# Inverting the diagonal blocks of the delta rule by block doubling instead of rank-one steps

## The chip, the core and the metric

The kernel runs on one core of a Trainium2 chip. The metric is the device time of one execution in microseconds. TensorE (PE) multiplies matrices, with weight loads (PEld) beside it; VectorE (DVE) and ScalarE (ACT) do the elementwise work; GpSimd (POOL) issues some DMAs; SyncE (SP) issues most of them.

## The reference, cut to what matters

Two transformer blocks run one after the other on 512 tokens of width 1024. The first block's mixer has a gated delta rule with four heads; the rest (projections, attention, two MLPs) the change does not touch. For each chunk of a head a unit lower triangular system is solved:

```
k_beta = k * beta
v_beta = v * beta
m = jnp.where(strict, jnp.einsum('bhnid,bhnjd->bhnij', k_beta, k) * lmask, 0.0)
a = m + jnp.eye(c, dtype=f32)
rhs = jnp.concatenate([v_beta, k_beta * jnp.exp(decay)[..., None]], axis=-1)
sol = lax.linalg.triangular_solve(a, rhs, left_side=True, lower=True, unit_diagonal=True)
u_c = sol[..., :dv]
w_c = sol[..., dv:]
...
def step(state, inp):
    qk_i, q_dec_i, k_dec_i, u_i, w_i, cd_i = inp
    v_new = u_i - jnp.einsum('bhck,bhkv->bhcv', w_i, state)
    o = jnp.einsum('bhck,bhkv->bhcv', q_dec_i, state) + jnp.einsum('bhij,bhjv->bhiv', qk_i, v_new)
    state = state * cd_i[..., None, None] + jnp.einsum('bhck,bhcv->bhkv', k_dec_i, v_new)
    return state, o
```

The kernel uses chunks of 128 tokens, so a head has four systems of 128x128, and it forms the inverse of `a` itself.

## The kernel before, in words

Weights come from HBM in tiles of 128x1024, are split into a rounded high part (ACT, L256) and the rest (VectorE, L257), and every projection is made of three matmuls (L275 to L277). Loads are issued on SP (L253); a load waits until the casts of an earlier tile have freed its buffer.

`deltanet` writes the four heads down between the projections that feed them and others that don't depend on them: the output projection of the other branch (`do_wa`) and the key and value projections of the memory attention (`next(mem)`, weights `xa_wk` and `xa_wv`). After head 3, `w_out1` (weights `w_out_b`) needs the output of all four heads; before it, `fins[3]` transposes head 3's output (L743) and splits it (L307, L308).

The order of the instructions on each engine is fixed when the program is built: a planner walks through the program with modelled durations and gives a free engine the earliest-written instruction that it takes to be ready. An engine then runs its list in that order. So instructions of two heads and of projections alternate on VectorE, and a change of one instruction can move others.

In `dn_head` the inverse is built in stages. L635 masks the scaled Gram matrix `M` to its diagonal blocks of 16. A product with an identity (L631) packs them into PSUM, and ACT copies them into `Lp` (L641), 16 columns for each of 128 rows and 4 chunks. Four DMAs on SP (L648), one a chunk, move them so that each of 32 partitions holds one whole block of 16x16 (`Lb`). There the inverse `Tb` starts as the identity (two memsets, L645 and L646), and 15 rank-one steps follow, two VectorE instructions each (L651 multiplies, L653 subtracts), every one dependent on the last. Four DMAs on SP (L655) bring `Tb` back to the rows, and L657 spreads it into `T_`. From there two more levels (16 to 32 and 32 to 64) and a last join to 128 are made with matmuls, VectorE and ACT, then the four chunks are run in sequence (L700 to L738). `Ob`, the scratch of the steps, lies in the tile `Mo`, which L635 fills with another mask when the steps are done.

Besides, from head 3 on, `sum_jobs` has ACT issue copies of 256 KB from HBM to HBM (L218) and GpSimd add to them (L222).

Of the kernel before, what the change touches and what calls it, by code (L numbers as in the profile page):

```python
# [12 lines left out]
AF = mybir.ActivationFunctionType  # L13
ALU = mybir.AluOpType
AX = mybir.AxisListType
# [50 lines left out]
class Kern:  # L66
# [491 lines left out]
    def dn_head(self, h, q, k, v, pr, gate, yb_h, yb_l):  # L558
        nc, mp = self.nc, self.mp
        V, TT = nc.vector, nc.vector.tensor_tensor  # L560
# [29 lines left out]
        r = self.rsqrt(mp, s2, 8, "dr")  # L590
# [34 lines left out]
        flat = lambda ap: ap.rearrange("p b c -> p (b c)")  # L625
        split = lambda ap, c: ap.rearrange("p b (o c) -> p b o c", c=c)

        def mmp(lhs, rhs, n):
            ps = psc()
            for b in range(NB):  # L630
                nc.tensor.matmul(ps[:, b * n:(b + 1) * n], lhs[:, b], rhs(b), start=True, stop=True)  # L631
            return vn_(ps, n)
# [5 lines left out]
        Md = masked(b4("dT"), "bd16")  # L638
        psL = mmp(Md, lambda b: self.bmask("ident16")[:, 0, :16], 16)
        Lp, Rp = b32("dVb")[:, :, :16], b32("dY")[:, :, :16]  # L640
        nc.scalar.copy(Lp, psL)  # L641
        Vt, Mo = b4("dV"), b4("dA" + e, 1)
        bl = lambda t, o: t[0:32].rearrange("p b c -> p (b c)")[:, o:o + 256].rearrange("p (r c) -> p r c", r=16)
        Lb, Tb, Ob = bl(Vt, 0), bl(Vt, 256), bl(Mo, 0)
        V.memset(Tb, 0.0)  # L645
        V.memset(flat(Tb)[:, 0::17], 1.0)  # L646
        for b in range(NB):
            nc.sync.dma_start(Lb[8 * b:8 * b + 8], Lp[:, b])  # L648
        for j in range(15):
            n, m = 15 - j, j + 1  # L650
            nc.vector.tensor_tensor(out=Ob[:, :n, :m], in0=Lb[:, m:, j:m].broadcast_to([32, n, m]),  # L651
               in1=Tb[:, j:m, :m].broadcast_to([32, n, m]), op=ALU.mult)
            nc.vector.tensor_tensor(out=Tb[:, m:, :m], in0=Tb[:, m:, :m], in1=Ob[:, :n, :m], op=ALU.subtract)  # L653
        for b in range(NB):
            nc.sync.dma_start(Rp[:, b], Tb[8 * b:8 * b + 8])  # L655
        T_ = b32("dTb")
# [1 line left out]
           in1=split(self.bmask("half"), 16).broadcast_to([P, NB, 2, 16]), op=ALU.mult)  # L658
        Md = masked(Md, "m16")
        masked(Mo, "m32")  # L660
        for lv, Mx in ((16, Md), (32, Mo)):
# [4 lines left out]
               in1=split(self.maskb("bd32"), 32), op=ALU.mult)  # L666
# [31 lines left out]
        o = b4("do", 1)  # L698
# [855 lines left out]
```

## Time and profile before

| | |
|---|---|
| median of 3 runs | 1709.44 us (1708.92 to 1714.01) |
| profiled execution | 1707.82 us, its span 1706.0 us |
| TensorE busy | 1681.1 us, 99% |
| VectorE, ScalarE, GpSimd busy | 1216.6, 822.0 and 66.3 us |
| mean granted TensorE clock | 0.996 |
| HBM read, written | 201.59 and 35.65 MB |

The span is the time from the first to the last instruction; the execution adds what lies around it. Times on the timelines count from the span's start. The ends of matmuls are modelled, so successive matmuls overlap in the listing; the distance between their starts is the rate.

### The profile page before, as it was taken

How to read it: one execution, taken by the hardware profiler on the slowest of the kernel's cores; microseconds unless marked ns; L12 is line 12 of the kernel's file. 1: busy time of each engine (PE TensorE's matmuls, PEld its weight loads, DVE VectorE, ACT ScalarE, POOL GpSimd, SP SyncE). 2: the span in 40 equal slices, each digit the busy share in tenths (PEclk: the TensorE clock that was granted, in tenths of full speed). 3: DMA queues.
4: the chain of work that ended last, by engine and by line, in shares of the span. 5: the costliest groups of instructions: out<-in, count | busy, mean ns of one | idle time of the engine just before them, and what ended most of it. 6: DMA issues, size and time to landing. Idle time of an engine off the chain costs nothing.

```text
span 1706.0 us, 25979 instructions
## 1 busy us (share of the span) xinstructions
PE 1681.1 (99%) x9924; PEld 1456.4 (85%) x9924; DVE 1216.6 (71%) x2574; ACT 822.0 (48%) x1462; POOL 66.3 (4%) x86
## 2 busy tenths in 40 slices
PE   9999999999999999999999999999999999999998
PEld 8988898877898989888988887788888989898987
DVE  6988885756686868688845569865556767676875
ACT  5355654544444444454444457654244444444553
POOL 0200001000000000000000000000000000000000
PEclk9999999999999999999999999999999999999999
DMA  6321357436546464423333332334464454643331
GB/s 202 100 75 53 104 162 182 112 93 171 122 134 165 131 167 131 130 93 107 100 91 101 99 87 68 93 87 118 116 188 128 132 166 131 166 131 123 100 111 50
DMA packets 81948, 205.64 MB, mean 121 GB/s; under 512 B 13088, under 2 KB 14240, under 8 KB 81824
## 3 DMA queue, kind: packets, MB, share of 16 engines
q1 hardware_dynamic: 62672, 169.29, 31.9%
q0 software_dynamic: 9216, 16.78, 6.9%
q10 hardware_dynamic: 9936, 17.91, 3.8%
q8 instruction: 78, 1.28, 0.3%
q14 instruction: 46, 0.38, 0.1%
HBM read 201.59 MB, written 35.65 MB: 139 GB/s over the span
## 4 chain that ended last, share of the span: by engine, by line
PE 88%; DVE 7%; ACT 2%; issue 1%; DMA 1%; SPq 0%; ACTq 0%; DVEq 0%
PE psd L276 21%; PE psd L275 21%; PE psd L277 21%; PE x L275 5%; PE x L276 5%; PE x L277 5%; DVE wl L257 1%; PE c L578 1%; PE c L631 1%; PE lg L1308 1%; PE po L1335 1%; ACT wh L256 1%; DVE acc L318 1%; DVE S L418 1%; PE m L1229 1%
## 5 line engine op out<-in xcount | busy, mean ns | idle before, releaser
L277 PE MATMUL psd<-S,wl 128*128 128x512 f32 (+1 forms) x1256 | 485.1, 387 | 0.6 <-DVE wl L257 0.5
L275 PE MATMUL psd<-S,wh 128*128 128x512 f32 (+1 forms) x1256 | 484.3, 386 | 0.8 <-ACT S L307 0.8
L276 PE MATMUL psd<-S,wh 128*128 128x512 f32 (+1 forms) x1192 | 459.6, 386 | 0.2
L275 PEld LDWEIGHTS psd<-S,wh 128*128 128x128 f32 x1256 | 237.2, 189 | 46.2 <-ACT S L307 1.0
L277 PEld LDWEIGHTS psd<-S,wl 128*128 128x128 f32 x1256 | 237.2, 189 | 45.8 <-DVE wl L257 1.4
L257 DVE TENSOR_TENSOR wl<-wr,wh 128x1024 fp32r<-128x1024 f32 (+2 forms) x160 | 192.0, 1200 | 107.6 <-ACT wh L256 107.0
L276 PEld LDWEIGHTS psd<-S,wh 128*128 128x128 f32 x1192 | 225.0, 189 | 43.4 <-DVE S L305 1.4
L256 ACT CAST wh<-wr 128x1024 fp32r<-128x1024 f32 (+2 forms) x160 | 164.0, 1026 | 160.3 <-PE psd L276 112.3
L276 PE MATMUL psd<-wl,S 128*128 128x256 f32 (+2 forms) x480 | 135.6, 283 | 0.3 <-DVE wl L257 0.3
L275 PE MATMUL psd<-wh,S 128*128 128x256 f32 (+2 forms) x480 | 135.5, 283 | 0.0
L277 PE MATMUL psd<-wh,S 128*128 128x256 f32 (+2 forms) x480 | 135.2, 282 | 0.0
L275 PE MATMUL x<-S,wh 128*128 128x256 f32 x452 | 128.0, 285 | 3.1 <-DVE x_fm L947 2.9
L276 PE MATMUL x<-S,wh 128*128 128x256 f32 x452 | 126.5, 281 | 0.0
L277 PE MATMUL x<-S,wl 128*128 128x256 f32 x452 | 126.0, 280 | 0.0
L276 PE MATMUL psd<-S,whx 128*128 128x512 f32 (+1 forms) x296 | 108.9, 368 | 0.1
L275 PE MATMUL psd<-S,whx 128*128 128x512 f32 (+1 forms) x296 | 107.9, 366 | 0.0
L277 PE MATMUL psd<-S,wlx 128*128 128x512 f32 (+1 forms) x296 | 107.2, 362 | 0.0
L947 DVE TENSOR_TENSOR x_fm<-x_fm,x 128x256 f32<-128x256 f32 x192 | 78.8, 417 | 27.3 <-PE x L277 27.1
L276 PEld LDWEIGHTS psd<-wl,S 128*128 128x128 f32 x480 | 90.4, 188 | 1.0 <-DVE wl L257 0.5
L275 PEld LDWEIGHTS psd<-wh,S 128*128 128x128 f32 x480 | 90.3, 188 | 0.4
L277 PEld LDWEIGHTS psd<-wh,S 128*128 128x128 f32 x480 | 90.5, 188 | 0.0
L275 PEld LDWEIGHTS x<-S,wh 128*128 128x128 f32 x452 | 84.9, 188 | 6.1 <-DVE x_fm L947 2.9
(465 smaller groups left out, 3180.4 us busy)
## 6 DMA issues: line engine op xcount, KB each, us to landing
wrx<-in_ffn_w_dram SPq DMA_DIRECT2D x32, 512.0 KB
wrx<-in_w_up_dram SPq DMA_DIRECT2D x20, 512.0 KB
wr<-in_w_in_qk_dram SPq DMA_DIRECT2D x16, 512.0 KB
sums_ffn_w<-in_ffn_w_dram ACTq DMA_DIRECT2D x32, 256.0 KB
wr<-in_ffn_w_dram SPq DMA_DIRECT2D x16, 512.0 KB
sums_w_down<-in_w_down_dram ACTq DMA_DIRECT2D x32, 256.0 KB
wr<-in_w_in_v_dram SPq DMA_DIRECT2D x12, 512.0 KB
wr<-in_w_up_dram SPq DMA_DIRECT2D x12, 512.0 KB
```

Source lines behind the costliest of these rows:

```text
L256: self.last_cast = nc.scalar.copy(hi[:, c], raw[:, c])
L257: nc.vector.tensor_tensor(out=lo[:, c], in0=raw[:, c], in1=hi[:, c].bitcast(F32), op=ALU.subtract)
L275: mm(ps, ah, bh, start=first, stop=False, skip_group_check=more)
L276: mm(ps, ah, bl, start=False, stop=False, skip_group_check=more)
L277: self.last_mm = mm(ps, al, bh, start=False, stop=last, skip_group_check=more)
L318: nc.vector.tensor_tensor(out=acc, in0=acc, in1=sq, op=ALU.add)
L418: nc.vector.tensor_scalar(out=d, in0=d, scalar1=ag[:, j, 0:1], scalar2=r[:, j:j + 1], op0=ALU.subtract, op1=ALU.mult)
L578: nc.tensor.matmul(blk(ps, b), lhs(b), rhs(b), start=True, stop=True)
L631: nc.tensor.matmul(ps[:, b * n:(b + 1) * n], lhs[:, b], rhs(b), start=True, stop=True)
L947: TT(out=x[n][t], in0=x[n][t], in1=ps, op=op)
L1229: nc.tensor.matmul(pX[:, :W], PT[:, tt], va[:, tt], start=True, stop=True)
L1308: nc.tensor.matmul(ps[:, i, K0:], qs[:, 2 * e2 + i, cs], kd[:, w, kc], start=(w == 0), stop=(w == 1))
```

## The change

The copy of the packed blocks gets the sign (-1). Of the four DMAs that lay out the blocks, two are now issued on SP and two on ACT. The 15 steps are replaced: blocks of 1 are joined to 2 by a copy of the entries below the diagonal, and then blocks of n = 2, 4 and 8 are joined to 2n, for all pairs of a block at once. For a pair, T21 = T22 (-L21) T11: each of the two products is a multiplication into `w` (n x n x n terms a pair, in n or m instructions, or one for n = 8) and a sum over the last axis. The right-hand factor is read transposed, so from element to element it moves by one row of 16 numbers. The four DMAs back stay on SP.

```
-        nc.scalar.copy(Lp, psL)
+        nc.scalar.activation(Lp, psL, AF.Copy, scale=-1.0)
         Vt, Mo = b4("dV"), b4("dA" + e, 1)
...
         for b in range(NB):
-            nc.sync.dma_start(Lb[8 * b:8 * b + 8], Lp[:, b])
-        for j in range(15):
-            n, m = 15 - j, j + 1
-            nc.vector.tensor_tensor(out=Ob[:, :n, :m], in0=Lb[:, m:, j:m].broadcast_to([32, n, m]),
-               in1=Tb[:, j:m, :m].broadcast_to([32, n, m]), op=ALU.mult)
-            nc.vector.tensor_tensor(out=Tb[:, m:, :m], in0=Tb[:, m:, :m], in1=Ob[:, :n, :m], op=ALU.subtract)
+            (nc.sync, nc.scalar)[b % 2].dma_start(Lb[8 * b:8 * b + 8], Lp[:, b])
+        V.tensor_copy(flat(Tb)[:, 16::34], flat(Lb)[:, 16::34])
+        for n in (2, 4, 8):
+            m = 8 // n
+
+            def part(t, o, i, j):
+
+                c = o + 17 * n * i if i == j else o + 16 * n
+                v = rows(t)[:, c:c + 34 * n * (m - 1) + 17 * n - 16]
+                return bass.AP(v.tensor, v.offset, [list(v.ap[0]), [34 * n, m], [16, n], [1, n]])
+
+            L21, T11, T22, T21 = part(Vt, 0, 1, 0), part(Vt, 256, 0, 0), part(Vt, 256, 1, 1), part(Vt, 256, 1, 0)
+            w = rows(Mo)[:, :m * n ** 3].rearrange("p (q i j k) -> p q i j k", q=m, i=n, j=n)
+            for lhs, rhs, out in ((L21, T11, L21), (T22, L21, T21)):
+                rT = rhs.rearrange("p q k j -> p q j k")
+                if n < m:
+                    for i in range(n):
+                        TT(out=w[:, :, i], in0=lhs[:, :, i:i + 1].broadcast_to([32, m, n, n]), in1=rT, op=ALU.mult)
+                else:
+                    for i in range(m):
+                        TT(out=w[:, i], in0=lhs[:, i].rearrange("p i (o k) -> p i o k", o=1).broadcast_to([32, n, n, n]),
+                           in1=rT[:, i:i + 1].broadcast_to([32, n, n, n]), op=ALU.mult)
+                V.reduce_sum(out=out, in_=w, axis=AX.X)
         for b in range(NB):
             nc.sync.dma_start(Rp[:, b], Tb[8 * b:8 * b + 8])
```

## Rows read from the trace of the kernel before

**Rows 1.** The page, busy time of each engine.
```profile
PE 1681.1 (99%) x9924; PEld 1456.4 (85%) x9924; DVE 1216.6 (71%) x2574; ACT 822.0 (48%) x1462; POOL 66.3 (4%) x86
```

**Rows 2.** Stretches: us, busy us of each engine, granted clock, DMA share, GB/s.
```profile
252.00:256.00 4.00, 4.00 (x37) 4.00 (x36) 4.00 (x21) 2.06 (x6) 0.81 (x1) 1.00 0.81 261
...
264.00:268.00 4.00, 2.72 (x22) 2.32 (x20) 3.24 (x6) 1.63 (x3) 0.47 (x1) 1.00 0.87 211
...
292.00:296.00 4.00, 2.24 (x9) 1.12 (x8) 1.97 (x12) 1.28 (x4) 0.45 (x1) 1.00 0.48 67
296.00:300.00 4.00, 3.22 (x8) 2.48 (x8) 1.34 (x2) 0.84 (x2) 0.00 (x0) 0.51 0.00 0
300.00:304.00 4.00, 4.00 (x13) 3.15 (x12) 3.68 (x6) 4.00 (x7) 0.00 (x0) 0.63 0.15 42
```

**Rows 3.** Timeline of PE: start, us, line, operation, count, idle before and its releaser.
```profile
224.32 1.16 PE L578 MATMUL c<-masks,slg 128*128 128x128 f32 x8 [1.46 <-ACT c L587]
...
267.82 1.08 PE L631 MATMUL c<-dTb,dT 128*128 128x32 f32 x8 [0.96 <-DVE dTb L657]
...
292.74 0.40 PE L277 MATMUL psd<-S,wl 128*128 128x512 f32 x1
294.90 1.20 PE L743 MATMUL c<-masks,do 128*128 128x128 f32 x4 [1.76 <-ACT do L738]
296.88 1.65 PE L275 MATMUL psd<-S,wh 128*128 128x512 f32 x3 [0.78 <-ACT S L307]
298.32 0.63 PE L276 MATMUL psd<-S,wh 128*128 128x512 f32 x1
...
302.99 0.40 PE L277 MATMUL psd<-S,wl 128*128 128x512 f32 x1
```

**Rows 4.** Timeline of ACT, head 3's copy of the packed blocks.
```profile
240.60 0.21 ACT L641 COPY dVb<-c 128x64 f32<-128x64 f32 x1
```

**Rows 5.** Timeline of SP, head 3's DMAs in and out.
```profile
240.84 2.67 SPq L648 DMA_DIRECT2D dV<-dVb  x4
...
261.92 2.68 SPq L655 DMA_DIRECT2D dY<-dV  x4
```

**Rows 6.** Timeline of DVE, head 3's steps and what follows them.
```profile
246.65 0.17 DVE L651 TENSOR_TENSOR dA<-dV 32x15 f32<-32x15 f32 x1
...
249.53 1.21 DVE L257 TENSOR_TENSOR wl<-wr,wh 128x1024 fp32r<-128x1024 f32 x1
...
261.68 0.16 DVE L653 TENSOR_TENSOR dV<-dV,dA 32x15 f32<-32x15 f32 x1
...
267.47 0.29 DVE L657 TENSOR_TENSOR dTb<-dY,masks 128x128 f32<-128x128 f32 x1 [0.76 <-DMA dY<-dV]
```

**Rows 7.** Groups by line, 110 to 280 us: count, busy us, mean ns, idle before.
```profile
L653 DVE TENSOR_TENSOR dV<-dV,dA 32x15 f32<-32x15 f32 (+7 forms) x60 | 11.4, 191 | 0.3
...
L651 DVE TENSOR_TENSOR dA<-dV 32x15 f32<-32x15 f32 (+7 forms) x60 | 11.3, 188 | 0.3
```

**Rows 8.** Groups by line and shape on DVE, whole span.
```profile
L257 DVE TENSOR_TENSOR wl<-wr,wh 128x1024 fp32r<-128x1024 f32 x146 | 179.0, 1226 | 105.0 <-ACT wh L256 104.4
...
L736 DVE TENSOR_TENSOR do<-do,gate 128x512 f32<-128x512 f32 x4 | 2.7, 678 | 0.0
L1169 DVE TENSOR_REDUCE rm<-E 128x4 f32<-128x512 f32 x4 | 2.7, 677 | 0.0
...
L653 DVE TENSOR_TENSOR dV<-dV,dA 32x15 f32<-32x15 f32 x8 | 1.3, 159 | 0.0
...
L651 DVE TENSOR_TENSOR dA<-dV 32x64 f32<-32x64 f32 x4 | 0.8, 206 | 0.0
```

**Rows 9.** Line 218, ACT's copies: min/median/max ns, first and last start.
```profile
L218 ACTq DMA_DIRECT2D sums_ffn_w<-in_ffn_w_dram x32: 497/497/612, 177.0 to 625.6; - x32
```

**Rows 10.** Waits of SP's queue, 100 to 300 us: total, times, longest.
```profile
SPq L253 <- DVE wl L257: 60.6, 12, 15.5
```

**Rows 11.** Chain that ended last, a piece: start, us, what.
```profile
217.49 5.38 DMA wr<-in_xa_wk_dram
```

More of the change, by code (lines that the diff above doesn't have):

```diff
@@ L640, in dn_head @@
         Lp, Rp = b32("dVb")[:, :, :16], b32("dY")[:, :, :16]
-        nc.scalar.copy(Lp, psL)
+        nc.scalar.activation(Lp, psL, AF.Copy, scale=-1.0)
         Vt, Mo = b4("dV"), b4("dA" + e, 1)
-        bl = lambda t, o: t[0:32].rearrange("p b c -> p (b c)")[:, o:o + 256].rearrange("p (r c) -> p r c", r=16)
-        Lb, Tb, Ob = bl(Vt, 0), bl(Vt, 256), bl(Mo, 0)
+        rows = lambda t: t[0:32].rearrange("p b c -> p (b c)")
+        bl = lambda t, o: rows(t)[:, o:o + 256].rearrange("p (r c) -> p r c", r=16)
+        Lb, Tb = bl(Vt, 0), bl(Vt, 256)
         V.memset(Tb, 0.0)
```

## The prediction

> **What bounds the kernel now.** I read the page first. TensorE is busy for 1681.1 of 1706.0 us [rows 1], so all other engines together can give back at most the 25 us in which it is not, plus what a slow clock costs. Vector work as such buys nothing; the question is where TensorE waits for the delta rule, and whether this change reaches that place.
>
> Second, the table by stage. The four heads run from about 105 to 297 us. TensorE is full through nearly all of it, because projections are interleaved with the heads' small products. It runs dry at the end of the last head: idle in 264 to 268, more so in 292 to 300, and the granted clock falls to 0.51 and 0.63 in the two stretches from 296 to 304 [rows 2]. [...]
>
> Third, the order of TensorE's work there [rows 3]. It stalls 0.96 us at 267.82 for VectorE's L657, the tile made from head 3's inverted blocks. Its other work ends at 293.14 (292.74 + 0.40); it stalls 1.76 us for head 3's last scaling and 0.78 us for the split of head 3's output. Then 14 matmuls of 128x512 take from 296.88 to 302.99, 6.11 us, eleven of them 0.427 us apart; at the 0.233 us of the rows after 302.99 they would take 3.27. So the clock costs 2.84 us. Altogether 0.96 + 1.76 + 0.78 + 2.84 = 6.3 us hang on how late head 3 is. The other heads end while projections still fill TensorE, and being earlier buys nothing directly.
>
> Fourth, head 3's own chain backward, on three engines. The blocks leave PSUM at 240.60 [rows 4]; four DMAs on SP take 2.67 us to issue [rows 5]; the first rank-one step starts at 246.65 and the last ends at 261.84 [rows 6]; four DMAs take 2.68 us to issue [rows 5] and the last lands 2.87 us later, when L657 starts at 267.47 [rows 6]. The 30 instructions of the steps thus stand in 15.2 us. In all heads they are 120 and 22.7 us [rows 7], 5.7 us for one head. So 9.5 of the 15.2 us is other work put between the steps: while one step waits for the one before it, the order written at build time lets something else go, at worst a weight cast of 1.2 us, as at 249.53 [rows 6].
>
> **The change, part by part.** VectorE. A head loses 30 instructions and gets 17: a copy; for n = 2 four products of 16 elements and two sums; for n = 4 four products of 64 and two sums over 128; for n = 8 two products of 512 and two sums over 512. Prices [rows 8]: 0.16 us for products and sums of 16 to 32 elements (the row of 15), 0.21 for 64 (the row of 64), 0.28 for sums over 128 (my estimate between the row of 64 and that of 512), 0.68 for 512, for product and sum alike. So 0.16 + (4 x 0.16 + 2 x 0.16) + (4 x 0.21 + 2 x 0.28) + (4 x 0.68) = 5.2 us, against 5.7: VectorE gains some 0.5 us a head, 2 us in all, hidden under TensorE. No row shows a read that jumps 64 bytes from element to element, as the right-hand factor does (it is read transposed). Its bounds: no more than an ordinary product, or twice the time, as if 1024 elements (1.23 us) [rows 8], plus 1.1 us a head. I take the lower end, since the row nearest in size is the product of 512.
>
> [...]
>
> What changes more is the depth. Thirty dependent steps become 13 levels (the products of a pair don't wait for each other): 12 gaps for other work instead of 29. With nothing in the gaps the chain takes 5.2 us and saves 10; with all of the 9.5 us still in them it saves 0.5. VectorE is full in this stretch (4.00 of 4 us at 252 to 256) [rows 2], and part of the other work belongs to head 2 and was written earlier, so it goes first. I take 6.5 us of other work, two thirds: 11.7 us, 3.5 saved.
>
> The transfer in. Two DMAs on SP and two on ACT instead of four on SP: half of 2.67, 1.3 us earlier. Bounds: a loss, if ACT's are held up by the ACT work ahead of them or share the queue with the 256 KB copies that ACT issues in this stretch (L218, 0.50 us each) [rows 9]; at best 1.3. I take 1.3, as the copy that feeds them runs on ACT directly ahead of them. ACT pays some 1.3 us a head, and what queues behind is the next casts. SP is free 1.3 us sooner for its weight loads. The transfer back is unchanged.
>
> [...]
>
> The sign moves into the copy at L641, which stays one ACT instruction (nothing). The scratch tile, its reuse by the mask at L635, and all that follows stay.
>
> Sum. L657 comes 3.5 + 1.3 = 4.8 us earlier (bounds 0.5 to 11.3, less with a late ACT). Then the 0.96 us stall goes; other work on TensorE ends at about 292.2; head 3's transposes could start at 290.1 instead of 294.90 and its output is ready at about 292.1. So the dry stretch (1.76 + 0.78) closes, and with it the slow clock (2.84): 6.3 us. Against it: the casts now between the steps go later. TensorE has no slack for them and the loads wait for them: SP stood 60.6 us for L257 to free the weight tiles [rows 10]. I charge one cast, 1.2 us, and 0.5 us for ACT's issues (my estimate, less than half of 1.3). Gain 6.3 - 1.7 = 4.6 us. The profiled execution took 1707.82 (span 1706.0 and 1.8 around it), 1.6 under the median; 4.6 off it is 1703.2, and off the median of 1709.44 it is **1704.8 us**.
>
> **The rivals.** *More than the end* (chance 0.20): fewer gaps let head 3 start sooner too, and the 1.46 us stall at 224.32 [rows 3], where ACT's squares are late, goes without a charge for casts. 6.3 + 1.5 = 7.8: 1701.6. For it: VectorE is the crowded engine in that stretch. Against: ACT's squares there stand behind a cast that waits for a weight load of 5.38 us [rows 11], which this change does not touch.
>
> *The gaps fill again* (0.20): nearly all of the other work stays between the steps, a wide product is no shorter than three small steps with fillers, and L657 comes 0.5 to 1.8 us earlier. Then the 0.96 us stall goes and little else; the clock still falls. Gain 1: 1708.4. For it: 9.5 of 15.2 us are others' work, and 5.2 against 5.7 is no saving. This is also the case in which doubling does not do what it says.
>
> *Casts too late, slower* (0.15): the short chain pushes the weight casts of 246 to 262 behind it. A load can't be issued until the cast frees its tile, so TensorE's filler starves for one load, 5.4 us [rows 11], and the clock falls as it does now, 2.8 us, with 0.96 gained: 1709.4 + 5.4 + 2.8 - 1.0 = 1716.6. It decides from the point at which a cast comes later than TensorE's next product needs it. For it: loads wait for casts [rows 10]. Against: by the end of the chain the same casts have all run, within the same stretch of VectorE.
>
> **How the numbers follow.** The forecast has 0.45, its own range 1703.1 (all 6.3) to 1707. A measurement can tell about 0.3%, 5.1 us, from no change. Faster than that are the first rival (0.20) and the better third of the forecast (0.17): 0.37. Slower is the last rival, 0.15. The rest, 0.48, is within. The range for 8 in 10 reaches down to 1699.5, past the first rival, and up to 1713, into the last one.
>
> **What would show it.** Head 3's L657 4 to 5 us earlier after its PSUM copy; VectorE's busy time lower by about 2 us; no stretch at half clock after head 3, and TensorE's idle before the output projection under 1 us. The products of 512 show the price of the 64-byte jumps. The prediction is wrong if the sum over 512 or its product takes well over 0.7 us, if L657 comes at the same distance from the copy as now, if the half-clock stretch stays with the chain shorter, or if TensorE's waits for L257 or for weight loads grow between 240 and 300 us.

## The result and the profile after

The changed kernel takes 1717.2 us at the median, against 1708.8 of the kernel before beside it. The ratio is 1.0043, 95% interval 1.0029 to 1.0057; one execution of 3876 us, of fourteen, is left out of it. By this ratio the change costs 7.4 us (8.4 by the medians); 4.6 us faster was forecast.

First the page of the changed kernel, for [rows 1]: TensorE's busy time grew by 7 us, with the same number of matmuls, and VectorE's by 4.

```profile
PE 1688.3 (98%) x9924; PEld 1462.8 (85%) x9924; DVE 1220.4 (71%) x2522; ACT 822.3 (48%) x1462; POOL 66.4 (4%) x86
```

Nearly all of it lies in the stage of the four heads. Its first projection and the first product of the attention scores behind it (timeline of PE) stand in the kernel before at

```profile
92.25 0.37 PE L275 MATMUL psd<-wh,S 128*128 128x260 f32 x1
...
327.80 0.28 PE L275 MATMUL sc<-S,S 128*128 128x256 f32 x1
```

and in the changed kernel, in whose timeline TensorE's larger waits are these, for [rows 3],

```profile
93.10 0.37 PE L275 MATMUL psd<-wh,S 128*128 128x260 f32 x1
...
218.83 0.39 PE L277 MATMUL psd<-S,wl 128*128 128x256 f32 x1 [0.62 <-DVE wl L257]
...
221.96 0.38 PE L277 MATMUL psd<-S,wl 128*128 128x256 f32 x1 [0.99 <-DVE wl L257]
...
256.12 0.50 PE L275 MATMUL psd<-wh,S 128*128 128x256 f32 x2 [0.49 <-ACT wh L256]
...
263.44 0.39 PE L275 MATMUL psd<-wh,S 128*128 128x256 f32 x1 [1.29 <-ACT wh L256]
...
271.62 0.50 PE L275 MATMUL psd<-wh,S 128*128 128x256 f32 x2 [1.94 <-ACT wh L256]
...
307.35 1.20 PE L761 MATMUL c<-masks,do 128*128 128x128 f32 x4 [1.68 <-ACT do L756]
309.33 1.12 PE L275 MATMUL psd<-S,wh 128*128 128x512 f32 x3 [0.78 <-ACT S L307]
...
339.06 0.28 PE L275 MATMUL sc<-S,S 128*128 128x256 f32 x1
```

so the stage ends 11.26 us later, which is the whole difference of the two spans (1717.3 and 1706.0); 0.85 of it was there when the stage began, a time that lies between 91.2 and 93.6 us over the profiles. (The 1.46 us wait at 224.32 is 1.09 now, at 224.80.) The dry end of head 3 (1.76 and 0.78 us before) is still there, 12.4 us later. New are the waits for weight casts ahead of it, two for VectorE's part (L257) and three for ScalarE's (L256), 5.3 us in all; from 200 to 300 us the kernel before has 0.3 us of such waits. Behind the longest of them, 1.94 us, the granted clock falls to 0.55 and 0.50, as the stretches show, for [rows 2] (us, busy us of PE, PEld, DVE, ACT, POOL, granted clock, DMA share, GB/s):

```profile
268.00:272.00 4.00, 2.06 (x18) 1.86 (x17) 0.89 (x2) 1.82 (x3) 0.36 (x1) 1.00 0.88 124
272.00:276.00 4.00, 3.93 (x20) 3.34 (x19) 2.69 (x5) 0.51 (x3) 0.00 (x0) 0.55 0.83 271
276.00:280.00 4.00, 4.00 (x20) 4.00 (x20) 0.30 (x2) 1.33 (x2) 0.81 (x1) 0.50 0.54 102
...
308.00:312.00 4.00, 3.22 (x10) 2.19 (x11) 1.38 (x2) 1.06 (x3) 0.00 (x0) 0.75 0.24 41
```

I add up such stretches of 4 us from 100 to 360 us for each profile: TensorE's idle time, and 4 us times what the granted clock lacks of 1. Before: 6.1 idle and 3.4 lost to the clock; after: 10.3 and 8.5. Over all runs the clock's part is less than in this profile: span times mean granted clock is 1707.6 us on average in the changed kernel and 1700.9 to 1701.6 in the series of the kernel before, at least 6 us more; the rest of the span, which the clock takes, is 7.3 us there and 5.7 to 7.4 in the kernel before. So the greater part of the loss is not the clock's, which adds 1.5 us at most on average, and the waits for casts, 5.0 us more, are the largest part of TensorE's idle time in the profile.

What holds TensorE up there is read from the chain that ended last, of the changed kernel (start, us, what):

```profile
248.05 0.95 ACT wh L256
249.02 1.23 DVE wl L257
250.27 4.67 DMA wr<-in_xa_wv_dram
255.02 1.06 ACT wh L256
256.10 1.23 DVE wl L257
257.35 4.92 DMA wr<-in_xa_wv_dram
262.35 1.05 ACT wh L256
263.43 1.24 DVE wl L257
264.68 5.76 DMA wr<-in_xa_wv_dram
270.52 1.05 ACT wh L256
271.60 1.24 DVE wl L257
```

From 248 to 273 us the kernel runs at the pace of one ring: ScalarE casts a weight tile (0.95 to 1.06 us), VectorE casts its rest (1.23 to 1.24 us), only then SP issues the next load into the tile (4.67 to 5.76 us), and ScalarE casts again. In the kernel before the chain of that stretch runs mostly through TensorE, and then through head 3's transfer back.

Head 3's chain, for [rows 4], [rows 5] and [rows 6], in the timelines of ACT,

```profile
244.89 0.25 ACT L641 ACTIVATE dVb<-c 128x64 f32<-128x64 f32 x1
```

of SP,

```profile
245.16 1.35 SPq L649 DMA_DIRECT2D dV<-dVb  x2
250.27 14.74 SPq L253 DMA_DIRECT2D wr<-in_xa_wv_dram  x5
265.30 2.68 SPq L673 DMA_DIRECT2D dY<-dV  x4
```

and of DVE (L675 is the old L657):

```profile
228.42 0.29 DVE L689 TENSOR_TENSOR dTb<-dTb,c 128x128 f32<-128x128 f32 x1 [0.77 <-PE c L631]
228.62 0.17 DVE L589 TENSOR_SCALAR dss<-dss 128x8 f32<-128x8 f32 x1
...
250.91 0.15 DVE L650 COPY dV<-dV 32x8 f32<-32x8 f32 x1
...
264.57 0.67 DVE L671 TENSOR_REDUCE dV<-dA 32x64 f32<-32x512 f32 x1
...
273.35 0.29 DVE L675 TENSOR_TENSOR dTb<-dY,masks 128x128 f32<-128x128 f32 x1 [0.53 <-DMA dY<-dV]
```

L675 comes 5.9 us later than L657 did (273.35 and 267.47). Piece by piece: the copy 4.3 later (244.89 and 240.60; 0.85 of it from the start of the stage); from it to the first step 6.02 us (6.05 before); the steps 14.33 (15.19); the issue back 2.68 (2.68); the landing 5.37 (2.87). So the chain of steps is 0.9 us shorter, and what was won is lost ahead of it and behind it. Head 3's first step, L589, which stood at 224.30 before, now stands behind head 2's L689, at 228.62, though its input, ScalarE's squares (L587), was there at 224.74. It is as late as the copy; e12 below shows that it is not the only reason why the copy is late.

Prices, groups by line and shape on DVE of the changed kernel, for [rows 8]:

```profile
L669 DVE TENSOR_TENSOR dA<-dV 32x512 f32<-32x512 f32 x8 | 8.2, 1030 | 0.0
L671 DVE TENSOR_REDUCE dV<-dA 32x64 f32<-32x512 f32 x8 | 5.3, 662 | 0.0
```

The sum is as predicted, the product 1.03 instead of 0.68.

### The profile page after: what moved, and what is told of

Its sections match the earlier page's. It is cut to its first block, busy times and chain, and to the rows that moved or that the text cites. A ratio compares the mean times of both kernels' runs of the same rounds, so it can differ in the third digit from the quotient of the medians.

```text
span 1717.3 us, 25922 instructions
## 1 busy us (share of the span) xinstructions
PE 1688.3 (98%) x9924; PEld 1462.8 (85%) x9924; DVE 1220.4 (71%) x2522; ACT 822.3 (48%) x1462; POOL 66.4 (4%) x86
## 4 chain that ended last, share of the span: by engine, by line
PE 86%; DVE 8%; ACT 3%; issue 2%; DMA 1%; ACTq 0%; DVEq 0%
PE psd L276 20%; PE psd L277 20%; PE psd L275 20%; PE x L275 5%; PE x L276 5%; PE x L277 5%; DVE wl L257 2%; PE c L631 1%; ACT wh L256 1%; PE c L578 1%; DMA wr<-in_xa_wv_dram 1%; PE lg L1326 1%; PE po L1353 1%; DVE e L361 1%; DVE S L418 1%
## 5 line engine op out<-in xcount | busy, mean ns | idle before, releaser
L257 DVE TENSOR_TENSOR wl<-wr,wh 128x1024 fp32r<-128x1024 f32 (+2 forms) x160 | 192.1, 1200 | 115.1 <-ACT wh L256 114.4
L256 ACT CAST wh<-wr 128x1024 fp32r<-128x1024 f32 (+2 forms) x160 | 164.0, 1026 | 154.7 <-PE psd L276 103.6
```

What stands on the lines that cost most here:

```text
L256: self.last_cast = nc.scalar.copy(hi[:, c], raw[:, c])
L257: nc.vector.tensor_tensor(out=lo[:, c], in0=raw[:, c], in1=hi[:, c].bitcast(F32), op=ALU.subtract)
```

## The experiments

Sixteen kernels. The order in which each engine takes its instructions is made when the program is built, from modelled durations, so an edit of the steps also changes the order of everything near them. Most runs separate the two. The theories: A, the new order costs; B, the new steps themselves cost; C, ScalarE's issuing of two DMAs costs. All results in one table (the stage begins between 91.2 and 93.6 us, so one or two us in its third column say nothing): ratio to the kernel before with its interval, head 3's copy (L641) and its L657 or L675, and idle and clock loss of TensorE from 100 to 360 us in the profile. These last columns, in us, are of one execution each, not always a typical one: e6's took 1720.2 us (median 1714.6), e5's 1714.7 (median 1718.5).

| kernel | ratio | copy, L657/L675 | idle, clock |
|---|---|---|---|
| before | 1 | 240.6, 267.5 | 6.1, 3.4 |
| changed | 1.0043 (1.0029-1.0057) | 244.9, 273.4 | 10.3, 8.5 |
| e1 new steps, old order | 1.0072 (1.0058-1.0086) | 251.1, 280.3 | 13.4, 5.2 |
| e2 old steps, new order | 1.0141 (1.0117-1.0164) | 263.1, 293.9 | 15.9, 25.6 |
| e3 two queues only | 1.0059 (1.0047-1.0071) | 243.1, 273.2 | 8.5, 12.0 |
| e4 doubling only | 1.0008 (0.9994-1.0021) | 237.1, 257.0 | 7.4, 0.0 |
| e5 doubling only, old order | 1.0045 (1.0028-1.0062) | 248.0, 277.0 | 12.3, 0.0 |
| e6 two queues, old order | 1.0021 (1.0006-1.0037) | 244.2, 273.3 | 10.2, 10.2 |
| e7 ScalarE padded, old order | 1.0025 (1.0007-1.0043) | 244.7, 273.5 | 10.8, 8.6 |
| e8 changed order, one queue | 1.0057 (1.0045-1.0070) | 243.9, 272.5 | 10.5, 8.6 |
| e9 changed, unit reads | 1.0060 (1.0036-1.0084) | 243.1, 272.7 | 11.9, 6.8 |
| e10 unit reads, one queue | 1.0009 (0.9996-1.0022) | 239.2, 259.3 | 7.9, 3.4 |
| e11 GpSimd's queue | 1.0033 (1.0020-1.0046) | 241.9, 266.8 | 6.8, 6.8 |
| e12 changed, front first | 1.0042 (1.0025-1.0059) | 243.2, 270.1 | 11.1, 5.1 |
| e13 doubling, front late | 1.0047 (1.0030-1.0064) | 251.3, 275.8 | 13.0, 5.1 |
| e14 before, front late | 1.0068 (1.0052-1.0083) | 249.2, 279.0 | 14.6, 10.2 |
| e15 doubling, scaling first | 0.9992 (0.9981-1.0004) | 238.3, 258.1 | 5.9, 1.7 |
| e16 as e15, unit reads | 0.9988 (0.9974-1.0002) | 238.2, 258.1 | 5.3, 1.7 |

**Steps and order, crossed (e1, e2).** Each instruction that both kernels share is given its neighbour in the other kernel's order, on each engine; nothing else changes.

```diff
+ORDER = {"SP": [...], "Activation": [...], "DVE": [...], "PE": [...]}
+def in_order(tc, nc):
+    for l in same_order(nc):
+        for a, b in zip(l, l[1:]):
+            tc.add_manual_dep(b, a.name, mybir.DependencyInfo(mybir.DependencyClass.NoSync, mybir.DependencyReason.DATA), reason="order")
```

> The changed kernel, instruction for instruction, with every instruction that both kernels share put in the order of the kernel before on SP, ScalarE, VectorE and TensorE (2455 of VectorE's, 422 of SP's, 1388 of ScalarE's, all 9554 of TensorE's); the new diagonal-block steps stand where their inputs allow. [...] Theory B (the loss comes from the steps themselves: two strided products at 1.02 us each where 0.68 was counted, and transfers issued by ScalarE): it stays, 1714 us or more, whatever the order. If it comes to 1704.8 the forecast's sum was right for the operations and wrong only for the order; at 1708.8 the shorter chain buys nothing even in the old order.

> The kernel before, its rank-one steps and its single queue kept, with every shared instruction in the order of the changed kernel. Theory A (order): it is slower than the kernel before by as much as the changed kernel is, about 1716 to 1720 us (its chain is 0.9 us a head longer than the new one, and nothing else is better). Theory B (the steps themselves): the order is worth nothing and it stays within 2 us of the kernel before, 1707 to 1711 us.

e1 came to 1.0072: the old order does not take the loss away, as it should by A, so A fell in that form. e2 came to 1.0141: the new order on the old steps costs 24 us, far more than the change. Neither order fits the other kernel's steps.

**The two parts alone (e3, e4).**

```diff
-            nc.sync.dma_start(Lb[8 * b:8 * b + 8], Lp[:, b])
+            (nc.sync, nc.scalar)[b % 2].dma_start(Lb[8 * b:8 * b + 8], Lp[:, b])
```

e3 is this line in the kernel before; e4 is the changed kernel with this line undone.

> The kernel before with the one edit that ScalarE issues two of the four inbound transfers of each head; rank-one steps kept; order left to the build. Theory A: the time follows the order that the build makes of it, not the queue: there one xa_wv weight load stands ahead of head 3's inbound transfers and the T-back transfers stand as before, so 1707 to 1713 us, and SP's issue of the pair takes 1.4 us instead of 2.67 for four. Theory C (the two extra issues on ScalarE, some 0.7 us each, delay its weight casts and so TensorE): slower than before by 2 us or more with waits of TensorE on the casts (wh, wl) in the stretch of head 3.

> The changed kernel with all four inbound transfers of a head back on SP; doubling kept; order left to the build. Its order on SP differs from both: head 3's inbound transfers stand ahead of the last xa_wk load, and six xa_wv loads stand behind its T-back transfers. Theory A: the time follows that order: head 3 ends early, so its own end costs little, but the casts of xa_wv come late; 1704 to 1716 us, read from whether TensorE waits on wh and wl after the T-back. Theory B (price of the steps): as slow as the changed kernel, 1715 to 1718 us. Theory C (ScalarE's issues): back to 1708 us or less.

The queue alone costs as much as the whole change; doubling alone costs nothing that can be told, and gains nothing. B in its plain form fell with e4. That spoke for C, but both have orders of their own, and e4's time lies in A's range too.

**The two parts in the order of before (e5, e6), and a dummy (e7).** e5 and e6 are e4 and e3 with the list above. e7 is the kernel before, in its own order, with

```diff
             nc.sync.dma_start(Lb[8 * b:8 * b + 8], Lp[:, b])
+            if b:
+                nc.scalar.copy(Vt[64:128], self.masks[64:128, :4])
```

> The changed kernel with all four inbound transfers on SP, and every instruction that it shares with the kernel before, the transfers included, in the order of the kernel before on all engines; the 17 new steps stand where their inputs allow (they end 14 to 25 VectorE places earlier than the 30 old ones). So the steps themselves are all that differs. Theory B (the steps are what costs): 1713 us or more, as in the first run of this series (1719.4, with ScalarE's issues). Theory C (ScalarE's issuing is what costs, the steps are worth nothing or a little): 1702 to 1709 us. If it comes to 1704.8 or less the forecast's gain by the shorter chain was there and was lost to the second queue.

> The kernel before, rank-one steps and all, in its own order on all engines; only the second and the fourth inbound transfer of each head are issued by ScalarE, two instructions behind the copy of the blocks, instead of by SP. Theory C: ScalarE stands still for 1.3 us at each head while it issues (seen as an idle 1.35 before the next ACTIVATE in the first run of this series), what it feeds comes late, and the time is 1712 us or more, as the two-queue kernel in its own order (1717.4). Theory A (that kernel lost by the build's order alone): 1706 to 1709 us, within 2 us of the kernel before.

> The kernel before, in its own order on all engines and with its single queue; ScalarE makes three added copies of 64x512 (about 0.46 us each, 1.4 us in all, into rows that are overwritten later) at each head, at the very place where it would issue the two transfers. It computes nothing that is used. Theory C (ScalarE's time at that place is what costs, not what the transfers do): as slow as the two-queue kernel in the same order, within 2 us. Theory D (it is the transfers, landing on another queue or out of step, not ScalarE's time): 1706 to 1710 us, as the kernel before.

e6 and e7 agree (1.0021 and 1.0025, both intervals just above 1): with the order held, it is ScalarE's time that costs, and not the transfers on another queue. Of e3's 0.59% that leaves the greater part to e3's own order. No run holds the order of the kernel before and changes nothing else, so what holding it costs by itself is not shown. In e6's timeline of ACT, at head 0, nothing on ScalarE starts while it issues (the last bracket: 1.66 us idle, "issue"):

```profile
117.25 2.20 ACTq L648 DMA_DIRECT2D dV<-dVb  x2
119.51 0.70 ACT L602 ACTIVATE slg<-masks,dg 128x128 f32<-128x128 f32 x2 [1.66 <-issue]
```

e7's three copies took more than I had reckoned, 1.91 us instead of 1.4 at head 3, so the dose is not quite equal.

e5 was a miss for me: doubling in the old order costs 0.45%; its profile has 6 us more of idle TensorE and no slow stretch. Head 3 is 7 us late there before its steps begin. One reason that I can show is what a step holds of VectorE. The listed durations overlap; in the kernel before (timeline of DVE)

```profile
214.32 0.21 DVE L651 TENSOR_TENSOR dA<-dV 32x64 f32<-32x64 f32 x1
214.46 0.14 DVE L182 TENSOR_TENSOR rsmt<-rsmy 128x2 f32<-128x2 f32 x1
214.56 0.21 DVE L653 TENSOR_TENSOR dV<-dV,dA 32x64 f32<-32x64 f32 x1
214.71 0.14 DVE L183 SCALAR_TENSOR_TENSOR rsmt<-rsmt,rsmv 128x2 f32<-128x2 f32 x1
```

a step of 0.21 us lets the next begin after 0.14 or 0.15. From each start to the next (without idle of over 0.2 us), from 100 to 300 us, the 120 old steps hold VectorE for 17.5 us, 4.4 a head, the 68 new ones of the changed kernel for 20.2, 5.0 a head (the listed durations add up to 5.7 and 6.0). The change adds 0.7 us of VectorE to each head where I had counted 0.5 off. Up to head 3's steps that is 2 us of the 7; for the rest no run shows a reason.

**Undoing parts in the changed order (e8, e9), and combinations (e10, e11).** e8 is e4 with the list of the changed kernel's order: the same instructions as e4 and e5, in a third order. e9 is the changed kernel with

```diff
-                        TT(out=w[:, i], in0=lhs[:, i].rearrange("p i (o k) -> p i o k", o=1).broadcast_to([32, n, n, n]),
-                           in1=rT[:, i:i + 1].broadcast_to([32, n, n, n]), op=ALU.mult)
+                        TT(out=w[:, i].rearrange("p i j k -> p i k j"), in0=lhs[:, i].rearrange("p i (k o) -> p i k o", o=1).broadcast_to([32, n, n, n]),
+                           in1=rhs[:, i:i + 1].broadcast_to([32, n, n, n]), op=ALU.mult)
```

e10 is e4 with the same edit; e11 is the changed kernel with `nc.gpsimd` in place of `nc.scalar`.

> The changed kernel, every instruction on every engine in the changed kernel's own order, with one thing undone: all four inbound transfers of a head are issued by SP again. Theory C (ScalarE's issuing costs): the 1.35 us for which ScalarE stands still at each head are gone; 3 to 6 us faster than the changed kernel, so 1711 to 1714 us against 1708 to 1710 of the kernel before. Theory A (the order alone makes it slow): 1716 to 1719 us, as the changed kernel, with TensorE's waits on the weight casts after 256 us still there.

> The changed kernel in its own order with two queues; only the wide products of the last two levels (n = 4 and 8) are laid out otherwise: both inputs are read at unit stride (or as one repeated value) and the output is written with jumps of 32 bytes (n = 8; 16 at n = 4). Theory B in the form that the 64-byte jumps of the read cost 0.35 us on each of the two 32x512 products: these fall from 1.03 to about 0.68 us, VectorE is occupied 0.7 us less at each head, and the time falls by 1 to 3 us, to 1713 to 1716. If writing with jumps costs as much, the products stay at about 1.0 us and nothing changes. If the products fall and the time stays at 1716 to 1719, their price isn't what costs.

> The doubling-only kernel (one queue, the order that the build made of it, which came to 1.0008 of the kernel before) with the unit-stride reads of the run before this. Its order is that kernel's. Theories B and C together: with both suspected costs gone it should be the fastest of all, 1703 to 1708 us, below the kernel before by 1 to 4 us. If the gain is taken back at the end of head 3 (its last scaling on ScalarE is still waited for, 2.7 us there), 1707 to 1711 us.

> The changed kernel with the second and fourth inbound transfer issued by GpSimd, which is nearly idle in this stretch, instead of by ScalarE; the order is the build's own. Theory C: without ScalarE's 1.35 us it is as fast as or faster than the one-queue kernel, 1706 to 1711 us, unless GpSimd's transfers themselves take longer than SP's. Theory E (a second queue brings nothing, whoever issues, and a transfer by GpSimd is slower): the steps start later than with SP alone and it is 1711 us or more.

e8 settles the changed kernel against C: with SP issuing all four again, in the same order, it stays at 1.0057. And e4, e5 and e8 are one program in three orders: 1.0008, 1.0045, 1.0057. ScalarE's waits for the xa_wv loads (waits of ACT, 200 to 300 us: total, times, longest) are in e8

```profile
ACT wh L256 <- DMA wr<-in_xa_wv_dram: 6.5, 4, 2.6
```

and in e4

```profile
ACT wh L256 <- DMA wr<-in_xa_wv_dram: 0.6, 1, 0.6
```

as they were 6.6 in the changed kernel and 1.0 before. That alone is not the whole of the ring: in e4 ScalarE also waits 4.1 us for xa_wk and 3.8 for w_out_b. What reaches TensorE are its own waits for casts (L256 and L257, same stretch): 0.3 us before, 0.7 in e4, 2.3 in e5, 3.2 in e8 and 5.3 in the changed kernel. So the order decides how long TensorE stands for the weight tiles.

e9: the product became no cheaper (groups by line, DVE),

```profile
L669 DVE TENSOR_TENSOR dA<-dV 32x512 f32<-32x512 f32 x8 | 9.0, 1124 | 0.0
```

so the layout with jumps in what is written (1.12 us) costs no less than the one with jumps in what is read (1.03 us), and no time was won. Both also repeat one operand, and no run has this product without jumps, so what the jumps alone cost is not shown. e10 repeats e4 in time as in order. e11 lies between e4 and the changed kernel: GpSimd issues the two transfers (0.60 to 0.82 us each) and ScalarE none, but the order is again another. Its time is in theory E's range, but not by E's reason: from copy to first step head 3 takes 5.1 us there and 6.4 in e4.

**One piece of the order (e12 to e14).** The only edit is a rule between two of VectorE's instructions; the build then fits the order of the rest around it. The two are head 3's first step (`front`, L589), and head 2's last part (`tail`, L675, or L689 in e13 and L671 in e14).

```diff
+    def before(self, a, b):
+        self.tc.add_manual_dep(b.ins, a.ins.name, mybir.DependencyInfo(mybir.DependencyClass.NoSync, mybir.DependencyReason.DATA), reason="order")
...
+        if h == 3:
+            self.before(front, self.ends[2])
```

e12 has it so, in the changed kernel; e13 (in e4) and e14 (in the kernel before) have `self.before(self.ends[2], front)`.

> The changed kernel with one rule of order added and nothing else: VectorE takes the first step of head 3 (L589, the sums of squares) before the last part of head 2's inversion (L675 to L689), as the kernel before and the doubling-only kernel do; the changed kernel takes it after. The build fits the rest around it. Theory F (the loss is head 3's late front: 4 to 5 us late there, 10 to 17 us late at L675): head 3's blocks are copied out some 4 us earlier than at 244.9, its L675 stands before 268, and the time falls by 5 us or more, to 1707 to 1712. Theory G (the loss lies in other places of the order, the weight loads behind the T-back transfers on SP, or in the two queues): 1715 to 1719 us as before this rule.

> The doubling-only kernel (one queue; 1710.9 us, 1.0008 of the kernel before) with the opposite rule alone: VectorE takes head 3's first step behind the last part of head 2's inversion. Theory F: it becomes as slow as the changed kernel, 1714 to 1719 us, head 3's copy at about 244 instead of 237.0 and its L675 at 265 or later instead of 257.0. Theory G: 1709 to 1713 us.

> The kernel before, rank-one steps and one queue, with the same rule as the run before this: head 3's first step behind the last part of head 2's inversion. Theory F: slower than the kernel before by 5 us or more, 1713 to 1720 us, with nothing of the change in it. Theory G: 1707 to 1711 us.

One late front, with what the build makes of it, brings e4 from 1.0008 to 1.0047 and makes the kernel before slower by 0.7% (1.0068), with nothing of the change in it. In e13 the front waits as the rule says, and head 3's copy comes 14 us later than in e4 (timeline of DVE):

```profile
233.33 0.29 DVE L694 TENSOR_TENSOR dTb<-dTb,c 128x128 f32<-128x128 f32 x1 [1.09 <-PE c L636]
233.54 0.16 DVE L594 TENSOR_SCALAR dss<-dss 128x8 f32<-128x8 f32 x1
```

But the loss comes by another road there than in the changed kernel. TensorE waits for the end of head 3, in e14 (timeline of PE)

```profile
310.52 1.35 PE L750 MATMUL c<-masks,do 128*128 128x128 f32 x4 [5.16 <-ACT do L745]
```

and 5.16 us in e13 as well, where the kernel before waits 1.76 and the changed kernel 1.68; for casts e13 waits 1.0 us and e14 1.9, the changed kernel 5.3.

e12 is the miss: the front went from 228.6 to 223.9, the copy only from 244.9 to 243.2, and the time stayed at 1.0042, with 4.3 us of waits for casts on TensorE. So a late front is enough for a loss of this size, but it is not shown to be the changed kernel's: setting it right there does not mend it, and which pieces of the order hold the loss stays open.

**Why an early inverse bought nothing (e15, e16).** In e4 head 3's L675 is 10.5 us earlier than before, and its closing transposes only 1.9 us (293.01 and 294.90). e4's timelines show the place, of DVE,

```profile
289.23 0.16 DVE L753 TENSOR_TENSOR dsc<-dsc,doy 128x4 f32<-128x4 f32 x1
```

of ACT,

```profile
291.61 1.04 ACT L256 CAST wh<-wr 128x1024 fp32r<-128x1024 f32 x1 [3.85 <-DMA wr<-in_w_out_b_dram]
...
292.56 1.28 ACT L756 ACTIVATE do<-do,dsc 128x128 f32<-128x128 f32 x4
```

and of PE:

```profile
293.01 0.62 PE L761 MATMUL c<-masks,do 128*128 128x128 f32 x2 [2.71 <-ACT do L756]
```

The last scaling, L756, had its input at 289.4, but stood in ScalarE's list behind a cast that waited 3.85 us for its weights.

```diff
+            if g == 1:
+                self.before(self.scaled_o, self.last_cast)
```

> The doubling-only kernel (one queue; 1.0008 of the kernel before; head 3's inverse 10 us earlier there, yet its end only 1.9 us earlier) with one rule of order: ScalarE does head 3's last scaling (L756) before the cast of the second w_out_b weights, not behind it. There the cast stood waiting 3.85 us for its load, and the scaling, ready at 289.3, began at 292.56. Theory H (the earlier end is lost behind that cast in ScalarE's list): TensorE's wait before the closing transposes, 2.71 us, goes to under 0.5, and the time falls by 2 to 3 us, to 1705 to 1708, at or below the kernel before. Theory I (the earlier end is worth nothing because the weights themselves come late): TensorE then waits as long for the cast or the load, and it stays at 1709 to 1712 us.

> The same rule in the kernel with unit-stride reads and one queue (1.0009 of the kernel before, 3.33 us of wait before the closing transposes), whose order is the same. Theory H: 2 to 3.5 us faster than without the rule, 1705 to 1708 us; theory I: as without it, 1709 to 1712 us. The two kernels should agree within 2 us.

Theory H held in the trace. In e15's timeline of ACT (L759 is the scaling) the order is turned,

```profile
290.61 1.28 ACT L759 ACTIVATE do<-do,dsc 128x128 f32<-128x128 f32 x4 [1.68 <-DVE dsc L756]
...
292.64 1.05 ACT L256 CAST wh<-wr 128x1024 fp32r<-128x1024 f32 x1 [0.40 <-DMA wr<-in_w_out_b_dram]
```

and TensorE's only wait over 0.15 us at the end of head 3 is

```profile
294.33 0.72 PE L275 MATMUL psd<-S,wh 128*128 128x512 f32 x2 [0.16 <-ACT S L307]
```

e15 and e16 take 1708.1 us each, beside 1710.1 of the kernel before: the fastest two, 0.16 and 0.21% under e4 and e10, and some 8 us (0.5%) under the changed kernel. A step of 0.16 to 0.21% is about as much as these intervals can tell. That they beat the kernel before is not shown: both intervals include 1.

## Why the prediction was wrong

**The bound.** Right: TensorE had 25 us to give, and every result above is read from its idle time and its clock. The place was not the whole of it: the loss lies in waits that the kernel before hardly has, ahead of the dry end.

**The step that failed** is the sum's "L657 comes 3.5 + 1.3 = 4.8 us earlier". It moved head 3 in a fixed surrounding. The edit made the build choose another surrounding: L675 came 5.9 us later, 4.3 of them before the blocks were even copied out and 2.5 in the landing of the transfer back. That the order can do this by itself is shown by e4, e5 and e8, the same instructions with L675 at 257.0, 277.0 and 272.5, and by e14 without any of the change. The other side of the sum failed with it: for casts that go later I charged 1.2 us, and TensorE's waits for casts grew from 0.3 to 5.3 us. Which pieces of the order make them late stays open.

**The depth**, 3.5 us for 13 levels in place of 30: 0.9 in the changed kernel at head 3. Its gaps still took 8.5 us of other work (14.33 less 5.86 of steps), where I took 6.5; before it was 9.5. The mechanism itself is there: in e4, with the same steps, head 3's stand in 9.28 us (timeline of DVE, first and last),

```profile
243.42 0.16 DVE L650 COPY dV<-dV 32x8 f32<-32x8 f32 x1
...
252.03 0.67 DVE L671 TENSOR_REDUCE dV<-dA 32x64 f32<-32x512 f32 x1
```

5.9 us less than before. How much other work falls into the gaps is again a matter of the order.

**The 17 instructions** at 5.2 us: their listed durations add up to 6.0 us a head, mainly since the wide product takes 1.03 us and not 0.68. I took the lower bound. And the listed time was the wrong measure: in VectorE's time held, the steps went from 4.4 to 5.0 us a head, so the sign of this term was wrong too. Why the product takes 1.03 us is not shown: e9, which jumps in the writes instead, took 1.12, so these runs don't show that the reads are the cause.

**The second queue**, 1.3 us: none of it reached the chain, 6.02 us from copy to first step against 6.05, because L650 stood behind other work of VectorE. With the order held it is next to nothing at every head: 4.56, 4.13, 4.59 and 6.02 us in the changed kernel, 4.55, 4.30, 4.60 and 6.01 in e8 with one queue. The charge for ACT, 0.5 us, was too low in the order of the kernel before, where e6 and e7 cost 0.2%, some 4 us; in the changed order, e8 beside the changed kernel, ScalarE's issues cost nothing that can be told.

**The 6.3 us at the end.** They were there, and e15 fetched the dry part: with L675 9.3 us early and one cast out of the way the waits of 1.76 and 0.78 went to 0.16. Its sum still came to the kernel before, because idle time appeared elsewhere, 0.76 us at 224.6, 0.66 at 256.2 and 1.56 at 321.0. That its 1708.1 us are the 1708.4 of the rival *the gaps fill again* is chance: that rival has the chain hardly shorter. Nor does the dry end hang on how late head 3 is alone, as the sum has it: in e11 L675 is only 0.7 us earlier than before (266.78), and the wait at the end is gone (timeline of PE),

```profile
302.10 0.33 PE L761 MATMUL c<-masks,do 128*128 128x128 f32 x1 [0.19 <-ACT do L756]
```

while its clock falls earlier, from 268 to 284 us, for 6.8 us.

**The rival that ended nearest** is *casts too late, slower* (1716.6, chance 0.15; measured 1717.2). Its ring of loads and casts is the chain shown above, and its 5.4 us for a load are close to the 5.0 us by which TensorE's waits for casts grew. Its reason, casts pushed behind the shorter chain, is not what happened: the steps are only 0.9 us shorter, and they begin 4.3 us later. It says that the clock falls as it does now, yet adds a second 2.8 us for that; in the profile the clock took 5.1 us more, on average 1.5 at most. So the mechanism of the loss was foreseen here, and the nearness of the two numbers is in part luck. I should have given it more than 0.15: [rows 10] showed loads that wait for casts, and TensorE without slack.

**The signs I had named** were the right ones. Three of those for "wrong" came true: a product well over 0.7 us, L675 at no shorter distance from the copy (28.5 us, 26.9 before), waits for weight loads between 240 and 300 us. VectorE's busy time rose by 3.8 us instead of falling by 2.

## What to carry to other kernels

Where a build orders the queues from modelled durations, an edit inside a full stage is also a new order of the whole stage: compare the orders first, and test an edit with the old order held as well as with its own (e4, e5 and e8, one program in three orders, took 1.0008, 1.0045 and 1.0057 of the kernel before). A critical chain that gets earlier need not pay: in e4 L675 came 10.5 us earlier and the closing transposes only 1.9, because the last scaling stood behind a cast that waited 3.85 us for its load; look for such an instruction in each list that the chain passes through. Replacing many short instructions by few wide ones is to be priced by the time from one start to the next, not by the listed durations (here 4.4 and 5.0 us a head from start to start, 5.7 and 6.0 listed).

## What was not expected of the hardware

How long the clock stays low does not follow from the idle time alone: e5's profile has 12.3 us of idle in the stage and no stretch below 1.00, the kernel before 6.1 us of idle and 3.4 us lost to the clock, e2 15.9 and 25.6.

The eight transfers that ScalarE issues for the heads of the changed kernel take 0.6 to 1.3 us each, and in seven of the eight it starts nothing else meanwhile; the pair at head 0 of e6 took 2.20 us. The issues of L218, 0.50 us, need not hold it: in e4 one begins at 283.05 and a cast at 283.26.

The last of the same four transfers back landed 2.87 us after its issue before and 5.37 in the changed kernel. In the changed kernel the issue of a weight load ended 0.3 us ahead of the four, before 1.9 us; whether that made the difference no run shows.
